# A two-layer decoder with 64 experts on one core: the second turn of a full half moves right behind the first gate/up product, and the weight refills are listed by the release of their rooms

## The chip, the cores and the metric

The kernel runs on one core of a Trainium2 chip. The metric is the device time of one execution in microseconds (us); smaller is better. The core has a matrix engine (TensorE, PE in the rows; PEld is its weight loads), a vector engine (VectorE, DVE), a scalar engine (ScalarE, ACT) and SyncE (SP), which here issues nearly all transfers. A transfer (DMA) runs beside the engines.

## The reference

Two layers, each an attention (differential in layer 0, latent in layer 1) and then a mixture of experts over 256 tokens of width 1024. Attention is not touched by the change. Of the experts:

```python
def hier_moe(h, w_group, b_group, w_expert, b_expert, w_gate, w_up, w_down):
    ...
    g_w, g_idx = lax.top_k(p_group, 1)                       # 1 of 8 groups
    ...
    e_w, e_idx = lax.top_k(jax.nn.softmax(e_logits, axis=-1), TOP_K)   # 2 of its 8 experts
    ...
    def body(e, acc):                                        # all 64 experts, width 256
        hid = jax.nn.silu(t @ w_gate[e]) * (t @ w_up[e])
        return acc + combine[:, e, None] * (hid @ w_down[e])
```

Each expert has 3 MB of float32 weights (1 MB each of gate, up and down), so that the two layers read 384 MB of expert weights, nearly all that the kernel reads.

## The kernel before

**Halves.** A layer's 64 experts are worked through in 16 halves of four experts, t = 0 to 15 (`LAST` = 15). For a half, 32 token slots per expert are gathered by a product with a 0/1 matrix `sel` (`Gather.places` makes the matrix on DVE, `Gather.rest` multiplies, L1270, and scales the result into `xg`, L334). Then come the gate/up product of four experts side by side (`into`, L1323, 64 matmuls), silu on ACT (L1328) and a multiplication on DVE (L1330), two transposes (L1335), the down product (`out_of`, L1349, 32 matmuls), a copy out of PSUM (`taken`, L1381), and a product with the transposed, weighted `sel` that puts the rows back to their tokens (`back`, L1389, with four additions into `xs` on DVE, L1354). The gather of half t+1 stands ahead of the down product of half t, and the `back` of half t behind the gate/up product of half t+1.

**Full halves.** Where an expert of the half has more than 32 tokens, the half needs a second turn with the same weights for slots 33 to 64 (`second`, inside `full`). One bit for each half is computed on the chip and read into a register of every engine (`path`), and every engine branches on it once in a half (L1449). Bit 16 says that an expert has more than 64 tokens; then `long_way` does the half in another way. Its branch (L1406) stands inside `second`, so that only full halves come to it; with this input the long way is never taken, but its code is jumped over. A branch hint (`mark_branch_hint_location`) on PE announces the jump over `second` of the next half.

**Rooms and refills.** Weights live in 10 rooms of 2 MB in SBUF. A unit is what one room holds: units 3p and 3p+1 are gate and up of the two experts of pair p, unit 3p+2 is both down weights. Unit n lies in the room that unit n-10 had (`RING`). A half uses six units: for half t, 6t, 6t+1, 6t+3, 6t+4 (gate/up) and 6t+2, 6t+5 (down). `order` lists the units to be loaded; `free(units)` says in the program that rooms are given up, and issues from `order` on SP as long as the head of the list has its room. SP's queue is in order: a transfer whose room is still in use holds up all behind it. Before the change `free` of the gate/up units stands in both ways of the branch on `path`: behind the second turn's gate/up product in a full half, and behind the down product in the others (where the transfers wait for the gate/up matmuls alone). `free` of the down units stands at the half's end.

Of the kernel before, what the change touches and what calls it, by code (L numbers as in the profile page):

```python
# [69 lines left out]
def trunk_kernel(  # L70
# [22 lines left out]
    def temp(cols):  # L93
        return work.tile([128, 512], F32, name="temp", bufs=3)[:, 0:cols]
# [1199 lines left out]
    def moe(layer, front):  # L1294
# [31 lines left out]
        def hidden(gu, weight=None):  # L1326
            sil, hid = temp(256), temp(256)
            ACT.activation(sil, gu[:, 0:256], AF.Silu)  # L1328
            if weight is None:
                DVE.tensor_mul(hid, sil, gu[:, 256:512])  # L1330
            else:
                DVE.scalar_tensor_tensor(hid, sil, weight, gu[:, 256:512], op0=OP.mult, op1=OP.mult)  # L1332
            tp = psum_bank()
            for k in range(2):
                PE.transpose(tp[:, 128 * k:128 * k + 128], hid[:, k::2], ident)  # L1335
            hdT = work.tile([128, 3, 128], F32, name="aT0")[:, 0:2, :]
            ACT.copy(hdT.rearrange("p k t -> p (k t)"), tp[:, 0:256])  # L1337
            return hdT
# [65 lines left out]
        def second(t, j, multiplied):  # L1404

            with tc.If(path >> 16):  # L1406
                long_way(t, j)
            this = Gather(front, j)
            this.places(t, 1)
            this.rest()  # L1410
            this.weighted(t)
            gu = into(t, j)
            ACT.copy(selT[:, 1 - j], this.turned())
            multiplied()
            y = out_of(t, hidden(gu))
            back(taken(y, lambda: temp(512)), selT[:, 1 - j])
# [21 lines left out]
        order[2:8] = order[3], order[4], order[2], order[6], order[7], order[5]  # L1438
        state = {"next": 0, "free": set()}
        def full(t, path, done):  # L1440

            mark = dict(state)

            def at_once():

                state.update(mark)
                done()

            with tc.If((path >> t) & 1, preferred_fallthrough_block=True, label=f"full{layer}_{t}") as more:  # L1449
                second(t, t % 2 if t < LAST else (t + 1) % 2, at_once)  # L1450
            with more.Else():
                at_once()
                if t < LAST:
                    tc.mark_branch_hint_location(f"full{layer}_{t + 1}", "LikelyTaken", engines=[PE.engine])

        this, ts = front.first, None
        with tc.manual_schedule(engines={e.engine for e in (PE, ACT, DVE)}):
            for t in range(LAST + 1):
                g, _, pairs = halves_of(t)
                if t == LAST:  # L1460
                    back(ts, selT[:, (t + 1) % 2])
                    full(t, path, lambda: None)

                    rows, weight = temp(256).bitcast(F32R).rearrange("p (b t) -> p b t", b=2), small("sums", 1)
                    this.weighted(t, sel[:, (t + 1) % 2])
                    ACT.copy(rows, this.turned())
                    DVE.tensor_reduce(weight, this.turned(sel[:, (t + 1) % 2]), axis=AX.XY, op=OP.add)
                    y = out_of(t, hidden(into(t, t % 2), weight), 4, lambda y, n: back_last(y, n - 1, rows) if n else None)
                    back_last(y, 3, rows)
                    free(units(g, pairs, "gu") | units(g, pairs, "d"))  # L1470
                    break
                gu = into(t, t % 2)
# [3 lines left out]
                hdT = hidden(gu)  # L1476
# [4 lines left out]
                ts = taken(y, lambda: prob().rearrange("p a t -> p (a t)")[:, 0:512])  # L1481
                if t + 1 < LAST:
                    this.weighted(t + 1)
                if t == 0:
                    path = nc.values_load(front.path[0:1, 0:1], min_val=0, max_val=2 ** 17 - 1)
                full(t, path, lambda: free(units(g, pairs, "gu")))
# [82 lines left out]
```

## Time and profile before

| | |
|---|---|
| median of 3 runs | 1233.47 us (1233.05 to 1235.77) |
| the profiled execution | 1237.15 us, of which the span is 1235.3 us |
| PE busy | 996.9 us, 81% of the span |
| DVE, ACT busy | 422.4 us, 229.1 us |
| read from HBM | 433.03 MB |
| mean granted TensorE clock | 0.924 of full |

A row of the timeline gives start, length, engine, line, operation, output and inputs, shape, count, and in brackets how long the engine sat idle before it and what ended that. A float32 matmul is recorded twice. SPq is SP's queue: its rows are the issue of transfers, which then run by themselves. PEq, PEldq and DVEq are the sequencers of PE and DVE.

### The profile page before, as it was taken

To read this page: it belongs to the slowest core of one execution; us is meant where nothing else is said; L and a number is where in the kernel's file an instruction comes from. 1 tells how busy PE (TensorE), PEld (TensorE's weight loads), DVE (VectorE), ACT (ScalarE), POOL (GpSimd) and SP (SyncE) were. 2 spreads that over 40 slices of the span, in tenths; PEclk is the share of its full clock that TensorE was granted. 3 is DMA by queue.
4 is the path that set the end of the run, shared out by engine and by line. 5 is a ranking of instruction groups with operands and counts; after the bars stand their busy time and mean duration, and the time that the engine had idled before them with its cause. 6 is when DMAs were issued, how large, how long until landed. Compare 5 with 4: busy or idle time off the path is not lost. (4 is left out here: it accounts for less than half of the span.)

```text
span 1235.3 us, 16593 instructions
## 1 busy us (share of the span) xinstructions
PE 996.9 (81%) x6544; PEld 552.7 (45%) x6544; DVE 422.4 (34%) x996; ACT 229.1 (19%) x594; POOL 1.3 (0%) x23
## 2 busy tenths in 40 slices
PE   8998888777777777777888999787777777799776
PEld 8897744343333333333438777443233333343332
DVE  6897622221111111111318876222111111122122
ACT  5565410000000000000016874000000000001000
POOL 0000000000000000000000000000000000000000
PEclk9998999898988888888999999999888888899888
DMA  9456871999999999999943386999999999969994
GB/s 350 184 214 250 329 288 72 427 424 425 425 425 425 426 425 426 425 425 425 408 194 120 134 316 283 369 425 425 425 426 426 425 426 425 426 266 375 425 424 175
DMA packets 78007, 435.92 MB, mean 353 GB/s; under 512 B 6960, under 2 KB 23088, under 8 KB 30128
## 3 DMA queue, kind: packets, MB, share of 16 engines
q1 hardware_dynamic: 77728, 434.02, 85.2%
q8 instruction: 86, 1.41, 0.4%
q14 instruction: 49, 0.40, 0.1%
q10 hardware_dynamic: 144, 0.09, 0.0%
HBM read 433.03 MB, written 1.05 MB: 351 GB/s over the span
## 5 line engine op out<-in xcount | busy, mean ns | idle before, releaser
L1323 PE MATMUL bank<-room,areaC 128*32 128x512 f32 x2240 | 349.7, 701 | 154.2 <-DMA room<-in_moe_w_up_dram 108.3
L1323 PEld LDWEIGHTS bank<-room,areaC 128*32 128x32 f32 x2240 | 108.6, 126 | 389.9 <-issue 373.7
L1354 DVE TENSOR_TENSOR xs<-xs,bank 128x512 f32<-128x512 f32 (+1 forms) x148 | 96.9, 658 | 482.3 <-PE bank L1389 477.2
L1349 PE MATMUL bank<-room,aT 128*32 128x512 f32 (+1 forms) x1160 | 131.6, 583 | 2.5 <-ACT aT L1337 2.5
L1389 PE MATMUL bank<-prob,val 128*128 128x512 f32 x240 | 108.1, 593 | 1.9 <-DVEq L1449 1.9
L1473 ACT COPY val<-bank 128x256 f32<-128x256 f32 x30 | 11.2, 373 | 508.2 <-PE bank L1291 508.2
L422 PE MATMUL bank<-room,areaB 128*128 128x256 f32 (+3 forms) x544 | 86.6, 311 | 4.1 <-DVE room L390 2.7
L334 DVE TENSOR_TENSOR areaC<-bank,pack 128x512 f32<-128x512 f32 x70 | 48.4, 691 | 111.4 <-PE bank L1270 111.4
L422 PEld LDWEIGHTS bank<-room,areaB 128*128 128x128 f32 x544 | 76.3, 193 | 9.0 <-DVE room L390 3.2
L1270 PE MATMUL bank<-val,areaB 128*128 128x128 f32 x576 | 71.5, 284 | 7.6 <-PEq L1406 3.2
L1270 PEld LDWEIGHTS bank<-val,areaB 128*128 128x128 f32 x576 | 67.9, 197 | 10.7 <-issue 10.4
L1270 PE MATMUL bank<-val,areaA 128*128 128x128 f32 x544 | 66.9, 282 | 4.5 <-DVE lg L1182 1.9
L1349 PEld LDWEIGHTS bank<-room,aT 128*32 128x32 f32 x1160 | 35.3, 112 | 70.7 <-issue 62.0
L1270 PEld LDWEIGHTS bank<-val,areaA 128*128 128x128 f32 x544 | 63.6, 196 | 6.3 <-issue 6.0
L390 DVE TENSOR_TENSOR room<-room,room 128x2048 fp32r<-128x2048 f32 (+4 forms) x33 | 62.4, 1897 | 6.5 <-ACT room L388 6.5
L1389 PEld LDWEIGHTS bank<-prob,val 128*128 128x128 f32 x240 | 43.3, 190 | 46.7 <-issue 46.7
L388 ACT CAST room<-room 128x2048 fp32r<-128x2048 f32 (+4 forms) x33 | 51.9, 1589 | 16.7 <-PE bank L1323 8.0
L1381 DVE COPY prob<-bank 128x512 f32<-128x512 f32 x30 | 20.7, 691 | 87.3 <-PE bank L1349 87.3
L1335 PE MATMUL bank<-ident,temp 128*128 128x128 f32 x70 | 17.6, 334 | 40.5 <-DVE temp L1330 37.2
L1381 ACT COPY prob<-bank 128x512 f32<-128x512 f32 x30 | 17.6, 586 | 155.4 <-PE bank L1349 155.4
L422 PE MATMUL bank<-room,areaA 128*128 128x512 f32 (+1 forms) x176 | 43.9, 393 | 2.0 <-DVE areaA L692 2.0
L1335 PEld LDWEIGHTS bank<-ident,temp 128*128 128x128 f32 x70 | 11.0, 206 | 66.7 <-DVE temp L1330 61.5
(245 smaller groups left out, 748.7 us busy)
## 6 DMA issues: line engine op xcount, KB each, us to landing
room<-in_moe_w_gate_dram SPq DMA_DIRECT2D x124, 1024.0 KB, 17.8
room<-in_moe_w_up_dram SPq DMA_DIRECT2D x124, 1024.0 KB, 19.3
room<-in_moe_w_down_dram SPq DMA_DIRECT2D x122, 1024.0 KB, 19.6
room<-in_diff_w_in_dram SPq DMA_DIRECT2D x11, 1024.0 KB, 10.8
room<-in_diff_w_out_dram SPq DMA_DIRECT2D x2, 2048.0 KB, 9.3
room<-in_moe_w_gate_dram SPq DMA_DIRECT2D x8, 512.0 KB, 14.8
room<-in_moe_w_up_dram SPq DMA_DIRECT2D x8, 512.0 KB, 13.6
room<-in_moe_w_down_dram SPq DMA_DIRECT2D x8, 512.0 KB, 10.1
```

The costliest lines, as they stand in the source:

```text
L334: DVE.tensor_tensor(dst, tp, gain[:, k0:k0 + n, None].to_broadcast([128, n, dst.shape[2]]), op=OP.mult)
L388: step(c + name)(lambda f=f: f(hi().bitcast(F32R), w()))
L390: step(c + name)(lambda eng=eng: eng.tensor_tensor(lo().bitcast(F32R), w(), hi(), op=OP.subtract))
L422: PE.matmul(out, a[k][x_].bitcast(F32R), b[k][w_].bitcast(F32R), start=first and j == 0, stop=last and j == n - 1)
L1270: PE.matmul(self.ps[kk][:, k, :], self.front.xn[:, tb, 4 * kk + k, :], self.sel[:, tb, :], start=tb + k == 0, stop=tb == 1, skip_group_che ...
L1323: PE.matmul(gu[M * c:M * c + M], x(k, slice(M * c, M * c + M)), w[:, :, k, :], start=k == 0, stop=k == 7)
L1335: PE.transpose(tp[:, 128 * k:128 * k + 128], hid[:, k::2], ident)
L1349: PE.matmul(y[n][M * c:M * c + M], hdT[:, k, M * c:M * c + M], w[:, k, ns], start=first and k == 0, stop=last and k == 1, skip_group_check ...
L1354: DVE.tensor_add(xs[:, tb, ns], xs[:, tb, ns], acc)
L1381: (ACT.copy, DVE.tensor_copy)[n](t, y[n])
L1389: PE.matmul(acc, rows[:, tb, :], t, start=True, stop=True)
L1473: ACT.copy(selT[:, t % 2], this.turned())
```

## The change

Four things change in the mixture of experts, in both layers. The first half of `hidden` (silu and multiplication) becomes `hidden_rows`, the second half (transposes and copy) `hidden_columns`. In each half the branch on `path`, with `second` in it, now stands right behind the gate/up product and `hidden_rows`, and ahead of everything else of the half; its product rows wait in the spare columns of the tiles that hold the rows of the half before. In `second` the branch over the long way moves behind the second turn's gate/up product and gets an else part and a hint of its own; `multiplied()`, the `free` of the gate/up units, is in both parts. `order` lists each half's six refills by release, the four that wait for gate/up rooms first and the two that wait for down rooms behind them; before, only six entries near the start were permuted, in another way. In the last half the second turn stands behind the first gate/up product too, where it stood ahead of it.

```diff
+        def hidden_rows(gu, weight=None, hid=None):
+            sil, hid = temp(256), temp(256) if hid is None else hid
             ACT.activation(sil, gu[:, 0:256], AF.Silu)
...
+        def hidden_columns(hid):
             tp = psum_bank()
...
-        def second(t, j, multiplied):
-            with tc.If(path >> 16):
-                long_way(t, j)
+        def second(t, multiplied):
+            j = (t + 1) % 2
+            tc.mark_branch_hint_location(f"long{layer}_{t}", "LikelyTaken", engines=[PE.engine])
             this = Gather(front, j)
             this.places(t, 1)
             this.rest()
             this.weighted(t)
-            gu = into(t, j)
+            hid = hidden_rows(into(t, j), None, held[1][:, 512:768])
+            with tc.If(path >> 16, preferred_fallthrough_block=True, label=f"long{layer}_{t}") as more:
+                long_way(t, j)
+                multiplied()
+            with more.Else():
+                multiplied()
+            hdT = hidden_columns(hid)
             ACT.copy(selT[:, 1 - j], this.turned())
-            multiplied()
-            y = out_of(t, hidden(gu))
+            y = out_of(t, hdT)
             back(taken(y, lambda: temp(512)), selT[:, 1 - j])
...
-        order[2:8] = order[3], order[4], order[2], order[6], order[7], order[5]
+        for t in range(LAST - 1):
+            order[6 * t:6 * t + 6] = (order[6 * t + n] for n in (0, 1, 3, 4, 2, 5))
...
                 if t == LAST:
                     back(ts, selT[:, (t + 1) % 2])
-                    full(t, path, lambda: None)
...
-                gu = into(t, t % 2)
+                gu = into(t, t % 2)
+                hid = hidden_rows(gu, weight, held[0][:, 512:768])
+                if t == 0:
+                    path = nc.values_load(front.path[0:1, 0:1], min_val=0, max_val=2 ** 17 - 1)
+                full(t, path, lambda: free(units(g, pairs, "gu")))
...
                 ACT.copy(selT[:, t % 2], this.turned())
                 if t:
                     back(ts, selT[:, (t + 1) % 2])
-                hdT = hidden(gu)
+                hdT = hidden_columns(hid)
...
-                full(t, path, lambda: free(units(g, pairs, "gu")))
                 free(units(g, pairs, "d"))
```

**SP's queue, from the end of half 0 to the full way of half 1 in layer 0.** Each row is one transfer of 1 MB (or two), named by the room that it fills. Before:

```order
L147 DMA room_75<-in_moe_w_gate_dram 128x2048
L147 DMA room_75<-in_moe_w_up_dram 128x2048
L1449 REGISTER_ALU x2
L1449 COMPARE_AND_BRANCH
...
L147 DMA room_78<-in_moe_w_gate_dram 128x2048
L147 DMA room_78<-in_moe_w_up_dram 128x2048
L143 DMA room_1642<-in_moe_w_down_dram 128x2048 x2
L147 DMA room_76<-in_moe_w_gate_dram 128x2048
L147 DMA room_76<-in_moe_w_up_dram 128x2048
```

The same place now:

```order
L147 DMA room_75<-in_moe_w_gate_dram 128x2048
L147 DMA room_75<-in_moe_w_up_dram 128x2048
L147 DMA room_76<-in_moe_w_gate_dram 128x2048
L147 DMA room_76<-in_moe_w_up_dram 128x2048
L1465 REGISTER_ALU x2
...
L147 DMA room_78<-in_moe_w_gate_dram 128x2048
L147 DMA room_78<-in_moe_w_up_dram 128x2048
L143 DMA room_1642<-in_moe_w_down_dram 128x2048 x2
L147 DMA room_1736<-in_moe_w_gate_dram 128x2048
L147 DMA room_1736<-in_moe_w_up_dram 128x2048
L143 DMA room_69<-in_moe_w_down_dram 128x2048 x2
```

Room 76 (unit 15, free once half 0 has done its down product) stood behind room 78 (unit 16, which waits for half 1's last gate/up product) and now stands ahead of it; all four units that wait for half 1's gate/up rooms are issued together.

**DVE, half 1 of layer 0, a full half's way.** `prob` and `temp` are row tiles, `val` is `sel`, `areaC` is `xg`. Before:

```order
L1354 TENSOR_TENSOR xs<-xs,bank 128x512 x4
L1330 TENSOR_TENSOR temp<-temp,bank 128x256
L1262 TENSOR_TENSOR val<-slot_no,pos 128x256
L334 TENSOR_TENSOR areaC<-bank,pack_81 128x4x128 x2
L1381 COPY prob<-bank 128x512
L1285 TENSOR_TENSOR val<-val,wt 128x256
...
L1262 TENSOR_TENSOR val<-slot_no,pos 128x256
L334 TENSOR_TENSOR areaC<-bank,pack_81 128x4x128 x2
L1285 TENSOR_TENSOR val<-val,wt 128x256
L1330 TENSOR_TENSOR temp<-temp,bank 128x256
```

The same half now:

```order
L1333 TENSOR_TENSOR prob<-temp,bank 128x256
...
L1262 TENSOR_TENSOR val<-slot_no,pos 128x256
L334 TENSOR_TENSOR areaC<-bank,pack_81 128x4x128 x2
L1285 TENSOR_TENSOR val<-val,wt 128x256
L1333 TENSOR_TENSOR prob<-temp,bank 128x256
...
L1387 COPY temp<-bank 128x512
L1360 TENSOR_TENSOR xs<-xs,bank 128x512 x4
L1465 UNCONDITIONAL_BRANCH x2
L1360 TENSOR_TENSOR xs<-xs,bank 128x512 x4
L1262 TENSOR_TENSOR val<-slot_no,pos 128x256
```

The second turn's selection (the first L1262) came behind the additions of the half before, the first turn's multiplication and the next half's gather; now it follows the first turn's multiplication at once, and what it was behind comes after the second turn's own additions.

**PE, the last half of layer 1.** L1291 transposes `sel`, `room_...` are the weights. Before:

```order
L1389 MATMUL bank<-temp,val 128x512 x4
L1449 UNCONDITIONAL_BRANCH x2
L1291 MATMUL bank<-ident,val 128x128 x4
L1323 MATMUL bank<-room_78,areaC 32x512
...
L1335 MATMUL bank<-ident,temp 128x128 x2
L1349 MATMUL bank<-room_9947,aT_18007 32x256 x2
```

Now:

```order
L1465 COMPARE_AND_BRANCH
L1588 BRANCH_PREFETCH_HINT
L1270 MATMUL bank<-val,areaA 128x128 x16
...
L1395 MATMUL bank<-temp,val 128x512 x4
L1465 UNCONDITIONAL_BRANCH x2
L1341 MATMUL bank<-ident,prob 128x128 x2
L1291 MATMUL bank<-ident,val 128x128 x2
L1355 MATMUL bank<-room_10106,aT_18321 32x256 x2
```

The first turn's 64 gate/up matmuls stood behind the branch; they now stand ahead of it, and only the transposes and the down product follow.

## Rows read from the trace of the kernel before

**Rows 1.** The page, 40 equal slices: busy tenths of the transfer engines

```profile
DMA  9456871999999999999943386999999999969994
```

**Rows 2.** Windows: stretch, length, busy PE, PEld, DVE, ACT, POOL; clock, DMA share, GB/s

```profile
186.00:213.00 27.00, 22.76 (x174) 12.18 (x172) 8.38 (x15) 2.28 (x7) 0.00 (x0) 1.00 0.08 22
213.00:630.00 417.00, 320.38 (x2003) 137.80 (x2004) 84.99 (x145) 23.58 (x58) 0.00 (x0) 0.91 1.01 424
1098.00:1118.00 20.00, 16.38 (x148) 7.42 (x144) 3.88 (x8) 1.62 (x4) 0.00 (x0) 1.00 0.28 105
1118.00:1214.00 96.00, 76.35 (x468) 31.63 (x464) 24.17 (x40) 5.81 (x14) 0.00 (x0) 0.89 1.01 423
```

**Rows 3.** Waits, all engines: who waits for what, us in total, times, longest

```profile
PE bank L1323 <- DMA room<-in_moe_w_up_dram: 108.3, 38, 5.2
```

**Rows 4.** Timeline of SP's queue, layer 0, halves 0 and 1

```profile
176.47 0.33 SPq L147 DMA_DIRECT2D room<-in_moe_w_gate_dram  x1
176.89 0.38 SPq L147 DMA_DIRECT2D room<-in_moe_w_up_dram  x1
210.82 0.33 SPq L147 DMA_DIRECT2D room<-in_moe_w_gate_dram  x1
```

**Rows 5.** Timeline of PE, layer 0, half 1

```profile
185.46 0.44 PE L1291 MATMUL bank<-ident,val 128*128 128x128 f32 x2
...
200.00 3.81 PE L1270 MATMUL bank<-val,areaB 128*128 128x128 f32 x32 [1.81 <-DVE val L1262]
203.74 7.07 PE L1323 MATMUL bank<-room,areaC 128*32 128x512 f32 x64
```

**Rows 6.** Timeline of SP's queue, layer 1, around the full half

```profile
1113.87 0.33 SPq L147 DMA_DIRECT2D room<-in_moe_w_gate_dram  x1
...
1120.10 0.33 SPq L147 DMA_DIRECT2D room<-in_moe_w_gate_dram  x1
```

**Rows 7.** Timeline of PE, layer 1: the full half and the half behind it

```profile
1088.41 0.44 PE L1291 MATMUL bank<-ident,val 128*128 128x128 f32 x2
...
1106.78 7.07 PE L1323 MATMUL bank<-room,areaC 128*32 128x512 f32 x64
...
1116.45 3.64 PE L1349 MATMUL bank<-room,aT 128*32 128x512 f32 x32 [0.52 <-ACT aT L1337]
1120.02 3.70 PE L1389 MATMUL bank<-temp,val 128*128 128x512 f32 x8
1123.65 7.07 PE L1323 MATMUL bank<-room,areaC 128*32 128x512 f32 x64
...
1135.98 3.83 PE L1270 MATMUL bank<-val,areaA 128*128 128x128 f32 x32
1139.74 3.64 PE L1349 MATMUL bank<-room,aT 128*32 128x512 f32 x32
```

**Rows 8.** Groups by line: count, busy us, mean ns, idle before

```profile
L1262 DVE TENSOR_TENSOR val<-slot_no,pos 128x256 f32<-128x256 bf16 x33 | 13.8, 418 | 0.6 <-DVEq L1406 0.6
L1328 ACT ACTIVATE temp<-bank 128x256 f32<-128x256 f32 x35 | 13.6, 389 | 9.5 <-PE bank L1323 9.5
```

**Rows 9.** Branches by line: ns min/median/max, first and last start

```profile
L1449 PEldq COMPARE_BRANCH  x35: 79/344/6334, 169.9 to 1205.2; - x35
L1406 PEldq COMPARE_BRANCH  x3: 3222/3892/5872, 195.9 to 1098.8; - x3
```

**Rows 10.** Timeline of PE, the last half of layer 0 and of layer 1

```profile
604.78 3.67 PE L1389 MATMUL bank<-prob,val 128*128 128x512 f32 x8 [0.96 <-DVEq L1449]
611.61 3.81 PE L1270 MATMUL bank<-val,areaB 128*128 128x128 f32 x32 [3.16 <-PEq L1406]
643.30 0.50 PE L1335 MATMUL bank<-ident,temp 128*128 128x128 f32 x2 [2.22 <-DVE temp L1332]
...
1204.81 3.67 PE L1389 MATMUL bank<-prob,val 128*128 128x512 f32 x8 [0.96 <-DVEq L1449]
1211.59 1.08 PE L1291 MATMUL bank<-ident,val 128*128 128x128 f32 x4 [3.11 <-PEq L1449]
```

More of the change, by code (lines that the diff above doesn't have):

```diff
@@ L1449, in full @@
             with tc.If((path >> t) & 1, preferred_fallthrough_block=True, label=f"full{layer}_{t}") as more:
-                second(t, t % 2 if t < LAST else (t + 1) % 2, at_once)
+                second(t, at_once)
             with more.Else():
@@ L1454, in full, with kept @@
                     tc.mark_branch_hint_location(f"full{layer}_{t + 1}", "LikelyTaken", engines=[PE.engine])
-        this, ts = front.first, None
+        def kept():
+            return prob().rearrange("p a t -> p (a t)")
+        this, ts, held = front.first, None, [kept() for _ in range(2)]
         with tc.manual_schedule(engines={e.engine for e in (PE, ACT, DVE)}):
@@ L1459, in moe @@
                 g, _, pairs = halves_of(t)
+                weight = None
                 if t == LAST:
                     back(ts, selT[:, (t + 1) % 2])
-                    full(t, path, lambda: None)
-                    rows, weight = temp(256).bitcast(F32R).rearrange("p (b t) -> p b t", b=2), small("sums", 1)
+                    weight = small("sums", 1)
                     this.weighted(t, sel[:, (t + 1) % 2])
+                    DVE.tensor_reduce(weight, this.turned(sel[:, (t + 1) % 2]), axis=AX.XY, op=OP.add)
+                gu = into(t, t % 2)
[3 more added lines that the diff above has]
+                full(t, path, lambda: free(units(g, pairs, "gu")))
+                if t == LAST:
+                    rows = temp(256).bitcast(F32R).rearrange("p (b t) -> p b t", b=2)
+                    hdT = hidden_columns(hid)
                     ACT.copy(rows, this.turned())
-                    DVE.tensor_reduce(weight, this.turned(sel[:, (t + 1) % 2]), axis=AX.XY, op=OP.add)
-                    y = out_of(t, hidden(into(t, t % 2), weight), 4, lambda y, n: back_last(y, n - 1, rows) if n else None)
+                    y = out_of(t, hdT, 4, lambda y, n: back_last(y, n - 1, rows) if n else None)
                     back_last(y, 3, rows)
-                    free(units(g, pairs, "gu") | units(g, pairs, "d"))
+                    free(units(g, pairs, "d"))
                     break
-                gu = into(t, t % 2)
                 ACT.copy(selT[:, t % 2], this.turned())
@@ L1475, in moe @@
                     back(ts, selT[:, (t + 1) % 2])
[L1476 removed]
+                hdT = hidden_columns(hid)
                 this = Gather(front, (t + 1) % 2)
@@ L1480, in moe @@
                 y = out_of(t, hdT)
-                ts = taken(y, lambda: prob().rearrange("p a t -> p (a t)")[:, 0:512])
+                held = [kept() for _ in y]
+                ts = taken(y, iter([h[:, 0:512] for h in held]).__next__)
                 if t + 1 < LAST:
                     this.weighted(t + 1)
-                if t == 0:
-                    path = nc.values_load(front.path[0:1, 0:1], min_val=0, max_val=2 ** 17 - 1)
-                full(t, path, lambda: free(units(g, pairs, "gu")))
                 free(units(g, pairs, "d"))
```

5 lines of the change are left out of this document (3 added, 2 removed).

## The prediction

> **What bounds the kernel now.** I first looked at where the transfer engines pause, since most of the span is reading weights. The page's 40 slices show them full from the 8th to the 20th and from the 26th to the 39th, low before and between, which is attention, and with two dents at the experts, the 7th and the 36th slice [rows 1]. The windows give the level of the full stretches, 424 and 423 GB/s, and the depth of the dents: 22 GB/s from 186 to 213 us in layer 0, 105 GB/s from 1098 to 1118 us in layer 1 [rows 2]. In the full stretches PE waits for weights (108.3 us over 38 waits [rows 3]), so there the rate of the transfers is the time: 1 MB takes 1.0486 MB / 424 GB/s = 2.47 us, a room 4.9 us, a half's 12 MB 29.7 us. What a dent lost is 27 x (1 - 22/424) = 25.6 us and 20 x (1 - 105/424) = 15.0 us. Every microsecond of a dent that is filled should end the kernel one microsecond earlier, as long as transfers stay the bound behind it.
>
> What the dents are, the branch rows say: the branch of L1406 is reached by full halves only, three times, the first at 195.9, the last at 1098.8 us [rows 9]; the one between is the last half of layer 0 (PE's wait for it, at 611.61 [rows 10]). So the dents are the two full halves that have halves behind them. SP issues nothing between 176.89 and 210.82 us [rows 4]: its head is a refill that waits for the full half's second gate/up product, which ended then (203.74 + 7.07 [rows 5]). In layer 1 it is freed at 1113.87 in the same way [rows 6], 0.02 us behind the end of the product (1106.78 + 7.07 [rows 7]).
>
> **The change, part by part.**
>
> *Earlier release of the gate/up rooms.* Before, from the end of the first gate/up product to the refill are 210.82 - 185.46 = 25.4 us in layer 0 [rows 4, 5] and 1113.87 - 1088.41 = 25.5 us in layer 1 [rows 6, 7]: a back product, transposes, the next half's gather, the first down product, a jump, the second gather and product. Now only these stand between: silu 0.39, a multiplication of the size of the selection, 0.42, the selection itself 0.42 [rows 8], about 0.5 for the engines' branches (half of the 0.96 us that PE waits for DVE at a branch [rows 10]; the bounds are 0 and 0.96), a gather of 203.74 - 200.00 = 3.7 us, and 7.1 us of product [rows 5]. That is 12.5 us, so the release comes 12.9 and 13.0 us earlier.
>
> *Refills by release.* In layer 0 unit 15 (4.9 us of transfers), whose room is free by 176 us, goes ahead of unit 16, which waits. The transfers so run dry 4.9 us later. In layer 1, where before the list is plain, everything freed by the half ahead has been issued by the time that the full half starts, before as after: nothing there. But behind the release four rooms (8 MB, 19.8 us) instead of two are now ready.
>
> *What is late next: the down rooms.* They now wait for the second turn's end and then the rest of the first. From the second gate/up product's end: 2.6 us to the down product (1113.85 to 1116.45), 3.6 and 3.6 us for it and its back product (to 1120.02 and 1123.65 [rows 7]); then 1.0 for the join of the branch (the 0.96 us above); 0.4 for the transposed selection [rows 5]; 3.6 for the back product of the half before (the row of the same form); 0.4 for what its additions leave of the transposes, 1.0 until DVE has done these additions and the selection, 3.8 and 3.6 us for gather and down product [rows 7]. Sum 23.6. The 8 MB last 19.8, so a new gap of 3.8 us opens in each of the two full halves. It is 0 if PE can overlap the waits, and some 10 if each of the joins and jumps costs what they did at worst; I take 3.8. In the half behind, the four down megabytes (9.9 us) cover its 7.1 us gate/up product, which frees the next four rooms, so I see no third gap.
>
> Layer 0: 12.9 + 4.9 - 3.8 = 14.0 us of 25.6. Layer 1: 13.0 - 3.8 = 9.2 us of 15.0.
>
> *The last half.* In both layers the 0.96 us branch wait ahead of its back product goes [rows 10], and 1.5 us come in behind half 14's gate/up product, where PE must now wait for silu and multiplication ahead of the branch. In layer 0, whose last half is full, the 3.16 us jump and the 2.22 us wait for the multiplication go too, and 1.7 us (silu to selection, as above) and a 1.0 us join come: 0.96 + 3.16 + 2.22 - 1.5 - 1.7 - 1.0 = 2.1 us gained. In layer 1 the 3.11 us jump [rows 10] goes behind the gate/up product, to where PE waits for the multiplication anyway, and about 1.0 us of weighting on DVE that the jump had covered shows: 0.96 + 3.11 - 1.5 - 1.0 = 1.6 us gained. Either could be 0, or 4 if the clock is better there.
>
> *All other halves* get a wait of some 1.5 us behind the gate/up product. Their cover is the transfers: a half without waits takes 1139.74 + 3.64 - 1123.65 = 19.7 us of PE [rows 7], now 21.2, against 29.7 of transfers. This 8.5 us is also what lets PE, which leaves the full half later against its transfers than before, catch up within two or three halves. Without cover it would be 1.5 x 29, over 40 us. SP has more branches and copies of the same transfers; it takes one copy and waits for rooms anyhow.
>
> Sum: 14.0 + 9.2 + 2.1 + 1.6 = 26.9 us. The profiled execution, 1237.15 us with 1.85 outside its span of 1235.3, would become 1210.3. It lay 3.7 us above the median of the runs, 1233.47; from that the forecast is 1206.6 us.
>
> **The rivals.**
>
> *The jump over the long way still costs.* Its branch on PE took 3.2 to 5.9 us [rows 9], which left PE idle for 1.8 and 3.2 us [rows 5, 10]. It now has a hint, and hinted jumps on L1449 took 0.34 us at the median; but one of 6.3 is in that row too, and the last half's jump idled PE for 3.11 us although half 14 had hinted it. It would come behind the release of the gate/up rooms, so it only delays the down rooms: about 3 us in each of three full halves, 9 us in all, 1216. [...]
>
> *The wait moves to the down rooms in earnest.* My 23.6 us is a sum with short waits; two joins, and PE's half clock behind a pause, could make it 30. Then 6.4 us more are lost in both full halves: 1219. Against it: the rows of the second turn stood nearly without gaps before [rows 7].
>
> *No second gap.* If the rest of the half is done within the 19.8 us, 7.6 us more are gained: 1199.
>
> *The dent in layer 0 gives nothing.* If PE, later against its transfers, frees the rooms of the next halves too late, layer 0's 14 us come back as small gaps: 1221. The 8.5 us of cover for each half speak against it.
>
> [...]
>
> **How the numbers follow.** Chances: the forecast 0.60, with a range of its own from 1201 to 1212; the jump 0.14; the down rooms 0.11; no second gap 0.08; layer 0 without gain 0.03; slower 0.04. From 1197 to 1220 everything but the last two and the tails is inside, some 0.85; the bounds of the last half's terms move little in that. A measurement here can tell about 0.2% (2.5 us) from no change. Only the slower case ends above that, and I keep 0.01 for an effect that cancels: faster 0.95, same 0.01, slower 0.04.
>
> **What would show it.** In layer 0's full half the refill's issue should come some 12.5 us behind the first gate/up product's end, with a short pause of the transfers ahead of it (some 7 us) and another of about 4 ahead of the down refills; in layer 1 a first pause of 2 us and a second of 4. All stretches behind should stand at 424 GB/s again at once. PE's branch over the long way should take well under 1 us; if it takes 3 or more, the first rival holds. If the second pauses are 8 us or longer, it is the second rival. I would be wrong altogether if the windows behind a full half fell below 400 GB/s for more than one half, or if the halves that aren't full showed transfers waiting for rooms.

## The result and the profile after

The changed kernel takes 1192.87 us (median of 4 runs, 1190.08 to 1195.65), the kernel before 1233.26 us on the same chip (4 runs, 1232.5 to 1235.77): ratio 0.9669, 95% interval 0.9639 to 0.9699. That is 40.4 us faster. The direction was forecast, but the size was not: 26.9 us were expected, and the time lies 4 us below the range of 1197 to 1220 us. The profiled execution took 1190.08 us, with a span of 1188.3 us and a granted clock of 0.941.

First the transfers, as in [rows 1, 2]: the page's 40 slices, and the windows around the two full halves (same columns).

```profile
DMA  9556868899999999999954387999999999999996
```

```profile
186.00:213.00 27.00, 23.85 (x148) 10.67 (x144) 8.33 (x13) 2.94 (x7) 0.00 (x0) 0.94 0.79 320
185.00:200.00 15.00, 13.30 (x87) 4.23 (x76) 2.62 (x5) 1.61 (x4) 0.00 (x0) 0.89 0.76 297
208.00:220.00 12.00, 12.00 (x115) 4.94 (x114) 2.41 (x4) 0.59 (x1) 0.00 (x0) 1.00 0.69 266
213.00:610.00 397.00, 301.71 (x2006) 134.08 (x2002) 84.06 (x143) 23.68 (x56) 0.00 (x0) 0.93 1.01 421
1060.00:1078.00 18.00, 16.52 (x130) 7.13 (x130) 4.06 (x7) 1.61 (x4) 0.00 (x0) 1.00 0.95 396
1086.00:1098.00 12.00, 12.00 (x115) 5.30 (x118) 2.41 (x4) 0.58 (x1) 0.00 (x0) 1.00 0.89 352
1098.00:1172.00 74.00, 61.81 (x418) 29.52 (x414) 20.93 (x35) 5.14 (x12) 0.00 (x0) 0.95 1.01 422
```

Where 22 GB/s stood there are now 320, and the dent of layer 1 has left the slices. Each dent has become two short pauses, as forecast: in layer 0 they cost 15 x (1 - 297/424) = 4.5 us and 12 x (1 - 266/424) = 4.5 us, 9.0 in place of 25.6; in layer 1 1.2 and 2.0 us, 3.2 in place of 15.0. Behind them the rate is at its level at once.

SP's queue in layer 0 [rows 4] shows why: the refills that wait for the gate/up rooms are issued at 189.33 us, those for the down rooms at 213.70.

```profile
171.85 0.38 SPq L147 DMA_DIRECT2D room<-in_moe_w_up_dram  x1
189.33 0.34 SPq L147 DMA_DIRECT2D room<-in_moe_w_gate_dram  x1
...
192.45 0.90 SPq L143 DMA_DIRECT2D room<-in_moe_w_down_dram  x2
213.70 0.33 SPq L147 DMA_DIRECT2D room<-in_moe_w_gate_dram  x1
```

In layer 1 [rows 6] the two releases now are:

```profile
1069.69 0.33 SPq L147 DMA_DIRECT2D room<-in_moe_w_gate_dram  x1
...
1092.15 0.33 SPq L147 DMA_DIRECT2D room<-in_moe_w_gate_dram  x1
```

PE's timeline around the full half of layer 0 [rows 5], from the end of half 0's product to half 2's:

```profile
159.53 0.41 PE L1291 MATMUL bank<-ident,val 128*128 128x128 f32 x2 [1.71 <-PEq L1465]
...
165.63 1.05 PE L1270 MATMUL bank<-val,areaB 128*128 128x128 f32 x7 [2.65 <-issue]
166.60 3.64 PE L1355 MATMUL bank<-room,aT 128*32 128x512 f32 x32
170.06 7.05 PE L1323 MATMUL bank<-room,areaC 128*32 128x512 f32 x64
178.48 3.84 PE L1270 MATMUL bank<-val,areaB 128*128 128x128 f32 x32 [1.37 <-DVE val L1262]
182.25 7.07 PE L1323 MATMUL bank<-room,areaC 128*32 128x512 f32 x64
190.72 0.48 PE L1341 MATMUL bank<-ident,prob 128*128 128x128 f32 x2 [1.40 <-DVEq L1420]
```

The gain by stretches. Each number is the difference of two times in PE's timeline: the end of layer 0's first gate/up product (before 162.65, after 157.82), the end of half 14's (591.15, 569.21), the start of layer 1's first L330 (655.61, 627.55), the start of its first gate/up product (766.74, 737.88), the end of half 14's (1191.19, 1148.87) and the end.

| stretch, us | before | after | gained | forecast |
|---|---|---|---|---|
| to layer 0's first gate/up product | 162.7 | 157.8 | 4.8 | 0 |
| layer 0, to half 14 (full half) | 428.5 | 411.4 | 17.1 | 14.0 |
| layer 0, last half (full too) | 64.5 | 58.3 | 6.1 | 2.1 |
| attention of layer 1 | 111.1 | 110.3 | 0.8 | 0 |
| layer 1, to half 14 (full half) | 424.4 | 411.0 | 13.5 | 9.2 |
| layer 1, last half | 44.1 | 39.4 | 4.7 | 1.6 |

The first row is code that the change doesn't touch. The versions below, all with the same code there, took 156.2 to 160.3 us, so the 4.8 us belong to the profiled execution of before, which lay 3.9 us above the median of its 4 runs. (That of the changed kernel lay 2.8 us below its median, so the two profiles differ by 47.0 us and the medians by 40.4.) Without that row 42.2 us are gained where 26.9 were forecast. The experiments ask where the surplus is from. Each was timed beside the kernel before on the same chip, whose median there was 1233.29 to 1235.87 us.

### The profile page after: what moved, and what is told of

Read it like the earlier page. It is cut to its first block, busy times and chain, and to the rows that moved or that the text cites. A ratio compares the mean times of both kernels' runs of the same rounds, so it can differ in the third digit from the quotient of the medians.

```text
span 1188.3 us, 16712 instructions
## 1 busy us (share of the span) xinstructions
PE 964.3 (81%) x6544; PEld 542.3 (46%) x6544; DVE 425.1 (36%) x996; ACT 231.7 (19%) x594; POOL 1.3 (0%) x23
## 5 line engine op out<-in xcount | busy, mean ns | idle before, releaser
L1323 PE MATMUL bank<-room,areaC 128*32 128x512 f32 x2240 | 330.6, 674 | 110.3 <-DMA room<-in_moe_w_up_dram 110.3
L1323 PEld LDWEIGHTS bank<-room,areaC 128*32 128x32 f32 x2240 | 101.1, 122 | 329.3 <-issue 315.1
L1333 DVE TENSOR_TENSOR prob<-temp,bank 128x256 f32<-128x256 f32 x33 | 13.9, 421 | 391.5 <-ACTq L1465 197.9
L1395 PE MATMUL bank<-prob,val 128*128 128x512 f32 x240 | 110.3, 602 | 2.8 <-issue 1.7
L1331 ACT ACTIVATE temp<-bank 128x256 f32<-128x256 f32 x35 | 13.4, 383 | 485.4 <-PE bank L1323 485.4
L1355 PEld LDWEIGHTS bank<-room,aT 128*32 128x32 f32 x1160 | 34.8, 110 | 68.8 <-issue 60.8
L1291 PE MATMUL bank<-ident,val 128*128 128x128 f32 x74 | 15.0, 284 | 44.7 <-DVEq L1465 29.6
```

Of the source, the lines that this page charges most:

```text
L1291: PE.transpose(tp[:, tb, :], (self.sel if sel is None else sel)[:, tb, :], ident)
L1323: PE.matmul(gu[M * c:M * c + M], x(k, slice(M * c, M * c + M)), w[:, :, k, :], start=k == 0, stop=k == 7)
L1355: PE.matmul(y[n][M * c:M * c + M], hdT[:, k, M * c:M * c + M], w[:, k, ns], start=first and k == 0, stop=last and k == 1, skip_group_check ...
L1395: PE.matmul(acc, rows[:, tb, :], t, start=True, stop=True)
```

## The experiments

### Two parts, each alone

**The new list alone** (the kernel before with it):

```diff
-        order[2:8] = order[3], order[4], order[2], order[6], order[7], order[5]
+        for t in range(LAST - 1):
+            order[6 * t:6 * t + 6] = (order[6 * t + n] for n in (0, 1, 3, 4, 2, 5))
```

> The kernel before with the new list of refills alone. Theory A (the gain is the two dents of the transfers, and the early release of the gate/up rooms fills them): only unit 15, 4.9 us of transfers, comes ahead in layer 0's dent, so about 5 us faster than before, 1228 us. Rival B (the list does the main work, since four rooms instead of two are refilled at each release): at least 15 us faster, 1218 or less.

1236.55 us, ratio 1.0014 (0.9994 to 1.0034): no difference, where even the smaller expectation was a gain of 5. In the trace layer 0 up to half 14 did get shorter, 428.5 to 424.5 us, but its last half took 68.8 us in place of 64.5 and layer 1's attention 114.0 in place of 111.1. In that last half the clock was lower (0.90 over 588 to 640 us, against 0.97 over 596 to 648 before), and the gather behind the jump took 6.67 us where it took 3.81 [rows 10]:

```profile
603.56 6.67 PE L1270 MATMUL bank<-val,areaB 128*128 128x128 f32 x32 [3.17 <-PEq L1406]
```

The mean clock of all twelve runs of this version was low too, 0.908 to 0.913, where the seventeen runs of the kernel before beside it had 0.921 at the median. Why the clock was lower stays open.

**The moved block alone** (the changed kernel with the old list, the same edit the other way round):

> The changed kernel with the old list of refills. Theory A: the release still comes early, but only 4 MB (layer 1) or 6 MB (layer 0) are listed ahead of the first room that waits for the down product, so the second pause grows by about 10 us in both layers and unit 15's 4.9 us are lost: 18 to 22 us slower than the changed kernel, 1211 to 1215 us. Rival C (the early release by itself does it, the list only matters for unit 15): 5 us slower, 1198.

1212.51 us, ratio 0.982 (0.9788 to 0.9852), 22 us of the 40, inside the range of the theory that the list is what keeps the down rooms from holding up the queue. The pauses are large again (windows):

```profile
180.00:195.00 15.00, 13.33 (x120) 5.38 (x118) 2.14 (x4) 1.61 (x4) 0.00 (x0) 1.00 0.42 156
205.00:216.00 11.00, 11.00 (x106) 5.50 (x108) 2.40 (x4) 0.58 (x1) 0.00 (x0) 1.00 0.35 127
1094.00:1108.00 14.00, 13.11 (x101) 6.96 (x103) 5.49 (x9) 0.96 (x2) 0.00 (x0) 1.00 0.18 56
```

In layer 1 the second pause costs 14 x (1 - 56/424) = 12.2 us, against 2.0 with the new list: at the earlier release only the two rooms ahead of a down refill could be filled. In layer 0 the two pauses cost 9.5 and 7.7 us, against 4.5 and 4.5, so there the second did not grow by the 10 us that the theory said, and the total fits better than its parts. So list and block are worth 0 and 22 us alone and 40 together. Only some half of the 22 is in the stretches up to half 14: by the profiles the block alone gained 8.0 us there in layer 0 and 2.2 in layer 1, and 5.9 and 4.5 in the last halves, nearly what it gains there with the list. In the same two stretches the list alone gained 4.0 and lost 1.4, and both together gained 17.1 and 13.5.

### The branch over the long way

**Back ahead of the second turn**, without else part and hint:

```diff
-            tc.mark_branch_hint_location(f"long{layer}_{t}", "LikelyTaken", engines=[PE.engine])
+            with tc.If(path >> 16):
+                long_way(t, j)
...
-            with tc.If(path >> 16, preferred_fallthrough_block=True, label=f"long{layer}_{t}") as more:
-                long_way(t, j)
-                multiplied()
-            with more.Else():
-                multiplied()
+            multiplied()
```

> The changed kernel with the branch over the long way back at the head of the second turn, without hint and else part. If the jump costs what it did before (PE idle 1.8 to 3.2 us), the second turn and both releases come 2 us later in each of three full halves: 4 to 7 us slower than the changed kernel, 1197 to 1200. If the wait for silu, multiplication and selection hides the jump: no difference, 1193.

1198.08 us, ratio 0.9708 (0.9676 to 0.9741), 5.2 us above the changed kernel, as expected. The jump took 5.7 to 7.2 us each time, and PE was idle for 5.35 us ahead of layer 0's second gather.

**Without the hint alone** (the first line of that diff left out):

> The changed kernel without the hint for the jump over the long way. If the hint is what makes the jump short (0.34 us in the changed kernel), it takes 3 us or more again, behind the release of the gate/up rooms, and the down rooms come 1 to 3 us later in two full halves and the end of layer 0 too: 3 to 8 us slower than the changed kernel, 1196 to 1201. If not, the same 1193.

1190.76 us, ratio 0.9648 (0.9617 to 0.9679): no difference. The branch row of each, with the hint, ahead of the turn, and without the hint:

```profile
L1420 PEldq COMPARE_BRANCH  x3: 336/345/366, 186.7 to 1067.0; - x3
```

```profile
L1414 PEldq COMPARE_BRANCH  x3: 5710/5794/7179, 174.6 to 1062.1; - x3
```

```profile
L1419 PEldq COMPARE_BRANCH  x3: 434/457/4160, 188.5 to 1072.3; - x3
```

So the place and the else part took the cost away, not the hint: two of the unhinted jumps took 0.43 and 0.46 us. The third, 4.2 us, stood in the last half of layer 0 and did not show in the time. Which of place and else part it was, these two runs don't tell.

### Jumps that the forecast left out

**Half 0 without a branch**, in the kernel before:

```diff
+            if t == 0:
+                at_once()
+                tc.mark_branch_hint_location(f"full{layer}_1", "LikelyTaken", engines=[PE.engine])
+                return
             with tc.If((path >> t) & 1, preferred_fallthrough_block=True, label=f"full{layer}_{t}") as more:
```

> The kernel before, with no branch in half 0 of either layer: half 0 has no second turn in this version, and with this input needs none. It prices the jump of half 0, which the forecast left out: PE idle for 4.8 us ahead of half 1's gate/up product in layer 0, and that product in 8.8 us instead of 7.1. Theory A (this jump was on the path of layer 0's dent, and the change shortened it by coming to it earlier, which is the 3.1 us by which layer 0's term was too small): half 1's product ends 5 to 6.5 us earlier and so does the kernel, 1227 to 1229 us. Theory B (it is covered): 1232 to 1235 us.

1228.63 us, ratio 0.9973 (0.9953 to 0.9993), 4.8 us faster, as Theory A had it. In the profile layer 0 up to half 14 took 421.5 us in place of 428.5. Half 1's product, in the kernel before and here:

```profile
176.75 8.77 PE L1323 MATMUL bank<-room,areaC 128*32 128x512 f32 x64 [4.79 <-PEq L1449]
```

```profile
165.48 7.05 PE L1323 MATMUL bank<-room,areaC 128*32 128x512 f32 x64
```

**The last half of layer 1 without a branch**, in the kernel before:

```diff
                     back(ts, selT[:, (t + 1) % 2])
-                    full(t, path, lambda: None)
+                    if layer == 0:
+                        full(t, path, lambda: None)
```

> The kernel before, with no branch in the last half of layer 1 (that half then has no second turn, and with this input needs none). Before, its hinted jump was slow and left PE idle for 3.1 us, and the 64 matmuls behind it took 9.5 us at a granted clock of 0.74, against 7.2 us at 1.00 in the changed kernel. Theory A (this jump is the whole of what the end of layer 1 gained): 5 us less, 1227 to 1229 us, and the stretch from half 14's gate/up product to the end goes from 44.2 to about 39 us. Theory B (the product there waits for weights, or the clock is low there whatever stands ahead): at most 2 us less, 1231 us or more.

1229.6 us, ratio 0.9974 (0.996 to 0.9988), 3.7 us faster, between the two expectations; the last stretch went from 44.1 to 39.9 us, which is nearly all that the change gained there, and that is Theory A. The product behind the jump, in the kernel before, here, and in the changed kernel:

```profile
1212.61 9.50 PE L1323 MATMUL bank<-room,areaC 128*32 128x512 f32 x64
```

```profile
1206.14 7.29 PE L1323 MATMUL bank<-room,areaC 128*32 128x512 f32 x64
```

```profile
1167.74 7.19 PE L1323 MATMUL bank<-room,areaC 128*32 128x512 f32 x64
```

**The last half of the changed kernel in its old form**, second turn ahead of the first gate/up product:

```diff
                 if t == LAST:
                     back(ts, selT[:, (t + 1) % 2])
+                    full(t, path, lambda: None)
...
-                full(t, path, lambda: free(units(g, pairs, "gu")))
+                if t < LAST:
+                    full(t, path, lambda: free(units(g, pairs, "gu")))
...
-                    free(units(g, pairs, "d"))
+                    free(units(g, pairs, "gu") | units(g, pairs, "d"))
```

> The changed kernel, with the last half of each layer as before: its second turn ahead of the first gate/up product. It prices the new form of the last half. Theory A (own milestones: 6.1 us in layer 0 and 4.7 us in layer 1 came from it, by a jump ahead of the product and the lower clock that the product had behind it): 1202 to 1204 us. Theory B (the forecast's 2.1 + 1.6 us, the rest being differences from one execution to the next): 1196 to 1197 us.

1194.5 us, ratio 0.9687 (0.9664 to 0.9711): below both expectations, on Theory B's side, and 2 us above the changed kernel, with intervals that overlap. Layer 0's last half took 61.6 us, 3.3 more than after, but layer 1's last stretch 39.7, as after. So in layer 1 the gain isn't the new form. PE did not wait for its jump there, although that stands ahead of the product as before: 1.53 us of idling ahead of the transposes, for DVE's weighting, in place of 3.11 us for its own sequencer, and the product took 7.20 us. What differs from before is the time between hint and branch. The hint for the last half stands in the else part of half 14's branch, which was at the end of half 14 and is now near its start. Rows of the kernel before, then of the changed one (the last start in each is that of layer 1's last half; the branches before are in [rows 9]):

```profile
L1564 PEldq BRANCH_PREFETCH_HINT  x28: 31/36/41, 176.2 to 1201.7; - x28
```

```profile
L1588 PEldq BRANCH_PREFETCH_HINT  x31: 31/31/45, 159.2 to 1146.0; - x31
L1465 PEldq COMPARE_BRANCH  x35: 79/422/5947, 155.5 to 1172.3; - x35
```

The lead was 1205.2 - 1201.7 = 3.5 us and is 1172.3 - 1146.0 = 26.3 us; in this version it was 17.7. Two runs of the kernel before tried the lead alone.

**Both hints in the else part of half 13:**

```diff
-                if t < LAST:
+                if t < LAST - 1:
                     tc.mark_branch_hint_location(f"full{layer}_{t + 1}", "LikelyTaken", engines=[PE.engine])
+                if t == LAST - 2:
+                    tc.mark_branch_hint_location(f"full{layer}_{LAST}", "LikelyTaken", engines=[PE.engine])
```

> The kernel before, with the hint for the last half's branch given one half earlier, in the else part of half 13 beside the hint for half 14. Before, that hint was executed at 1201.7 us and the branch at 1205.2 us, 3.5 us later, and the jump took 6.1 us; in the changed kernel 26.3 us lie between them (1146.0 and 1172.3 us), and the jump takes under 1 us. Theory A (it is the lead of the hint that the change lengthened, and two hints can be pending): the last half's jump takes under 1.5 us, the stretch from half 14's gate/up product to the end goes from 44.2 to about 40 us, the time to 1229 to 1230 us; in layer 0 the last half is full and nothing changes. Theory B (only one hint is kept): one of the two jumps, of half 14 or of the last half, takes some 6 us, and the time stays at 1232 to 1234 us. Theory C (the lead has nothing to do with it): the last half's jump still takes some 6 us and half 14's is as short as before.

1234.89 us, ratio 1.0 (0.9974 to 1.0026): no gain. The hint led by 33 us (1169.1 to 1202.5 us), and the last half's jump still left PE idle for 3.31 us; at half 14's PE waited 0.96 us for DVE, as before. That is the outcome of both Theory B and Theory C.

```profile
1209.17 1.09 PE L1291 MATMUL bank<-ident,val 128*128 128x128 f32 x4 [3.31 <-PEq L1449]
1210.19 9.41 PE L1323 MATMUL bank<-room,areaC 128*32 128x512 f32 x64
```

**Half 14 without a branch**, so that one hint leads by 29 us with no jump between:

```diff
+            if t == LAST - 1:
+                at_once()
+                tc.mark_branch_hint_location(f"full{layer}_{LAST}", "LikelyTaken", engines=[PE.engine])
+                return
             with tc.If((path >> t) & 1, preferred_fallthrough_block=True, label=f"full{layer}_{t}") as more:
```

> The kernel before, with no branch in half 14 of either layer (it then has no second turn, and with this input needs none). The hint for the last half stands at the head of the block behind half 13, so some 33 us ahead of its branch, and no other jump lies between, as it does in the changed kernel (26.3 us). Theory A (a hint acts if it has time and no other jump comes between): the last half's jump takes under 1.5 us, PE's idle time of 3.1 us ahead of the transposes goes, the 0.96 us at half 14's branch too, the stretch from half 14's gate/up product to the end of layer 1 goes from 44.2 to about 39 us, the time to 1227 to 1230 us. Theory C (it depends on where the code lies or on the transfers beside it): the jump still takes some 6 us, the stretch only loses the 0.96 us, the time is 1231 us or more.

1231.63 us, ratio 0.9956 (0.9931 to 0.9981), 4.2 us below the kernel before, which took 1235.87 us on that chip; the time by itself lies in Theory C's range, the difference and the rows are Theory A's. The last stretch went to 38.6 us. Hint, branch, and PE in the last half:

```profile
L1568 PEldq BRANCH_PREFETCH_HINT  x26: 31/36/41, 171.7 to 1172.4; - x26
L1453 PEldq COMPARE_BRANCH  x33: 79/339/6424, 165.5 to 1201.5; - x33
1205.02 0.41 PE L1291 MATMUL bank<-ident,val 128*128 128x128 f32 x2 [0.93 <-DVEq L1453]
...
1205.95 7.25 PE L1323 MATMUL bank<-room,areaC 128*32 128x512 f32 x64
```

PE no longer waits for its own sequencer, only 0.93 us for DVE's, and the product is at 7.25 us. With one hint, 29 us of lead and no jump between, this jump did not hold PE up; with 3.5 us of lead it did for 3.11 us, and with 33 us, another hint beside it and another jump between, for 3.31 us. Each of these edits moves the code as well, so that the place of the code has a part in it isn't ruled out.

**What the long jumps have in them** is in the traces. Beside the weights they show small transfers on queues called instruction. The view of transfers over the last half's jump of layer 1 in the kernel before (1205.19 to 1211.28 us) has one of 16 KB on queue q8:

```profile
q8 instruction: 1, 0.02, 1.0%
```

Over the same jump in the changed kernel (1172.28 to 1172.62 us) it has none. In the profiled executions of the two kernels such a transfer starts inside every one of PE's 14 branches that took 3 us or more (8 before, 6 after), and the branch ends 2.2 to 2.6 us behind its start; it starts inside none of the other 62, which took at most 1.2 us. That the jump waits for this transfer is not shown; the rows show that the two come together. Behind 53 of the 59 hints the next such transfer began 2.9 to 3.6 us later. In the kernel before the one behind the last hint came at 1204.8 us, 0.4 us ahead of the branch, and another fell into the jump, at 1208.9.

### Without second turns

Both kernels with the code of the full halves set to zero; the rows in slots 33 to 64 are not computed:

```diff
-            DVE.tensor_add(code, code, top)
+            DVE.tensor_tensor(code, code, code, op=OP.subtract)
```

> The kernel before, with the code of the full halves set to zero: no second turn is done, and the rows in slots 33 to 64 are left out. Beside the next run it shows what the change does outside the full halves. The dents (25.7 and 15.3 us by bytes) go, and some 23 us of second turn in the last half of layer 0: 1168 to 1174 us.

> The changed kernel with the same left out: no second turn, rows in slots 33 to 64 not computed. Theory A (outside the full halves the change gains only where a slow jump became a fast one, and that depends on where the code of the halves comes to lie): 2 to 8 us below the run above. Theory B (the forecast's terms for the last halves without a second turn, 1.6 us in each layer): 3 us below it. Rival C (the wait behind each gate/up product costs somewhere): the same or slower than the run above.

1173.87 us (ratio to the whole kernel before 0.9524, 0.9502 to 0.9546), inside what was expected, and 1165.53 us (0.9444, 0.9426 to 0.9462). So 8.3 us are gained with no full half at all, a little more than Theory A allowed and far more than the forecast's 3.2. By stretches they lie in the last halves: layer 0's went from 46.4 to 38.4 us and layer 1's from 44.2 to 39.5, while the two stretches up to half 14 changed by 0.2 and 1.6 us. Attention of layer 1 gave 4.2 us back (109.3 to 113.5). With full halves the change gained 40.4 us; the 32 us between hang on second turns, if the two parts add up, which is only roughly so: layer 0's last half gained 8.0 us here and 6.1 with its second turn.

### Further versions

**Gather behind the down product**, in the changed kernel:

```diff
                 this.places(t + 1, 0)
-                this.rest()
                 y = out_of(t, hdT)
                 held = [kept() for _ in y]
+                this.rest()
```

> The changed kernel, with the next half's gather product moved from ahead of the down product to behind it. Theory (what is left of the dents is the late down rooms): the down rooms come free one gather (3.8 us) and one wait for the selection (0.9 us) earlier, so the second pauses, 4.5 us in layer 0 and 2.1 us in layer 1, go, less some 0.5 us each, since PE now waits for the copy of the transposes with nothing to do: 1186 to 1188 us, against 1192.9. Rival (the pauses are set by the gate/up rooms of the half behind, or the regular halves lose their cover): 1192 us or more, with the windows behind the full halves below 420 GB/s.

1189.44 us, ratio 0.9644 (0.9621 to 0.9667), between the two expectations and with an interval that overlaps the changed kernel's. The second pauses went as expected (394 GB/s from 208 to 220 us, 427 from 1086 to 1098), and the stretches to half 14 lost 2.7 and 3.3 us. But layer 1's last stretch grew by 2.9, since half 14's jump, though hinted, left PE idle for 2.93 us, where in the changed kernel PE waited 1.33 us for DVE:

```profile
1147.90 0.66 PE L1291 MATMUL bank<-ident,val 128*128 128x128 f32 x2 [2.93 <-PEq L1465]
```

**Hints for half 0 and behind a full half**, in the changed kernel:

```diff
                 second(t, at_once)
+                if t < LAST:
+                        tc.mark_branch_hint_location(f"full{layer}_{t + 1}", "LikelyTaken", engines=[PE.engine])
...
+                if t == 0:
+                    tc.mark_branch_hint_location(f"full{layer}_0", "LikelyTaken", engines=[PE.engine])
                 gu = into(t, t % 2)
```

> The changed kernel, with a hint for the branch of half 0 (which has none, and leaves PE idle for 1.7 us and then 2.7 us in layer 0) and for the branch of the half behind a full one (3.7 us idle). The scheduler puts the hint for half 0 at the head of the block that ends in that branch, in layer 0 the head of the program, some 150 us ahead of it. Theory A (a hint that far ahead still acts): the first gate/up product of half 1 ends some 4 us earlier, the first pause of layer 0 (4.5 us) nearly goes, 1188 to 1189 us. Theory B (it does not act so far ahead): only the half behind a full one changes, which transfers cover: 1192 to 1193.5 us.

1192.32 us, ratio 0.9666 (0.9645 to 0.9688): the time is Theory B's, the stretch Theory A's. With the hint for half 0 PE no longer waited for its own sequencer behind half 0's product: it was idle there for 1.59 us, for DVE's, where the changed kernel has 1.71 us for its own and then 2.65. Half 1's product began at 166.77 us in place of 170.06, and layer 0 to half 14 took 407.1 us. What the hint behind a full half did is not shown. The gain came back elsewhere: 1.2 us in layer 0's last half, 2.6 in the attention behind it, 3.7 in layer 1's end, where half 14's jump left PE idle for 3.05 us. The attention's share may be chance: over the sixteen profiles, whose work there is the same, it took 109.3 to 114.0 us.

**The gather's move and the hint for half 0 together:**

> The changed kernel with two additions that each moved its own stretch in the runs above: the next half's gather product behind the down product, and a hint for the branch of half 0. Theory (the gains are in different pauses of the transfers and add up): layer 0 from the first gate/up product to that of half 14 goes from 411.4 us (changed kernel) to about 404 us (each alone 408.7 and 407.1), layer 1's stretch stays near 408, and the time is 1184 to 1187 us. Rival (the jump in the last half of layer 1 comes back slow, as it did in both versions, and takes 3 us): 1187 to 1190 us.

1193.69 us, ratio 0.9674 (0.9653 to 0.9695), above both expectations: they don't add up. Layer 0 to half 14 took 407.3 us, not 404, and half 14's jump in layer 1 left PE idle for 2.87 us. No version was shown to beat the changed kernel.

## Why the forecast was too small

**What held.** The release came 189.33 - 177.11 = 12.2 us behind the first product in layer 0 and 12.1 in layer 1, forecast 12.5. The down rooms came 24.4 and 22.5 us behind the second product (213.70 and 1092.15 us in SP's queue), forecast 23.6, so the second rival's 30 is out. The half clock behind a pause that it names is in the trace of before: 0.50 from 177 to 179 us, behind 4.79 us of idling. The second pauses were 4.5 and 2.0 us, forecast 3.8. The other halves paid nothing: the windows show 421 and 422 GB/s behind the full halves and a clock of 0.93 and 0.95, above that of [rows 2]. No run shows the slower kernel that the forecast gave 0.04. "No second gap" is out as well, and so is "the dent in layer 0 gives nothing": that stretch gained 17.1 us. The first rival did not come: the jump would still cost 5.2 us ahead of the second turn, but where it now stands it takes 0.34 to 0.37 us.

**Layer 0's full half, 17.1 against 14.0.** The step that failed is its starting point: everything ahead of half 1's first product was taken as unchanged. Half 0's branch has no hint, and its jump of 6.25 us left PE idle for 4.79 us ahead of that product, which then took 8.77 us at a clock of 0.82. With the branch earlier in half 0 the jump began while half 0's product still ran (155.5 us, against 157.8) and took 3.57 us; half 1's product was back at 7.05, at 1.00. From half 0's product to the end of half 1's were 185.53 - 162.65 = 22.9 us; now they are 177.11 - 157.82 = 19.3. These 3.6 us make the first pause 4.5 us in place of the forecast 7. Half 0 without its branch shows that they are on the path.

**Layer 1's full half, 13.5 against 9.2.** The terms that were mis-sized are the two pauses: they account for 15.0 - 3.2 = 11.8, since they were 0.8 and 1.8 us shorter than forecast. The other 1.7 us aren't seen in the pauses and stay open; the same stretch gained 1.6 us without any second turn, and versions with the old code there differ by up to 1.4 us (424.4 to 425.8).

**The last halves, 10.8 against 3.7.** This is the largest miss, beyond even the bound of 4 for either. The step that failed is the clock of the products behind the waits, which the sum put at nothing. In layer 1 PE's waits from half 14's product to the end shrank from 7.45 to 5.61 us: 1.8, near the forecast 1.6. The rest is the product behind the jump, 9.50 against 7.19 us, and the transposes ahead of it. Windows over that product, before (behind 3.11 us of idling and four transposes) and after:

```profile
1212.60:1222.10 9.50, 9.50 (x65) 2.27 (x64) 0.42 (x1) 0.11 (x1) 0.00 (x0) 0.74 0.29 111
```

```profile
1167.70:1175.00 7.30, 7.23 (x66) 3.53 (x64) 0.42 (x1) 0.03 (x1) 0.00 (x0) 1.00 0.86 330
```

The clock was 0.74 and is 1.00; in the four transposes ahead of the product it was 0.50 before. The forecast also moved the jump to a place where PE waits anyway and left it its length. That the jump, whose hint the move of half 14's branch also moved, shrank from 6.1 us to 0.34 was luck: at 6.1 us it would have ended at 1178.4, some 2.3 us behind the start of the transposes at 1176.07 (an estimate from these rows). In layer 0 the waits from half 14's product to the first L330 shrank from 13.3 to 9.4 us, 3.9 where 2.1 were forecast, and the first down products behind the last transposes, before and after, went from 3.51 us at a clock of 0.54 to 1.93 us at 1.00:

```profile
644.27 3.51 PE L1349 MATMUL bank<-room,aT 128*32 128x256 f32 x32 [0.46 <-ACT aT L1337]
```

```profile
618.09 1.93 PE L1355 MATMUL bank<-room,aT 128*32 128x256 f32 x32
```

No run takes the parts of layer 0's last half one by one: its old form gave back 3.3 of the 6.1 us, and the rest is read from the rows alone.

Surplus by these steps: 3.1 + 4.3 + 4.0 + 3.1, and 0.8 in attention, 15.3 us in the profiled executions; 13.5 by the medians.

**Still open:** why hinted jumps are sometimes long (5.95 us at 327.1 us in the changed kernel, with 30 us of lead, where the transfers run on at 425 GB/s; half 14's in the last three versions, with PE idle for 2.93, 3.05 and 2.87 us), although a 16 KB transfer began 3.2 us behind the hint of the one at 327.1 us, as behind those of short ones; and why the new list alone gives its 4 us back.

## What to carry to other kernels

A queue in order is worth what its head allows: up to half 14 of the two layers earlier release alone gained 8.0 and 2.2 us, a list by release alone 4.0 and -1.4, and both together 17.1 and 13.5, so cost such a pair as one edit. When a branch moves, list what its hint and its neighbours' hints are now ahead of; a jump on the path cost its own idle time here (3.11 us in the last half of layer 1) and, in some places, a lower clock of the product behind it (0.74 there, 9.50 us in place of 7.19). Count from the last point that the edit really leaves alone, not from the first that it is meant to change.

## What was not expected of the hardware

With a hint for half 0's branch, PE was idle behind half 0's product for 1.59 us in place of 1.71 and 2.65 us in the changed kernel; with a hint 3.5 us ahead the last half's jump of layer 1 took 6.1 us in the kernel before. In the traces of both kernels each of PE's 14 jumps of 3 us or more has a 16 KB transfer that starts inside it, and none of the 62 shorter ones has. An idle time of PE of some 3 us at the last half's jump of layer 1, with only four transposes behind it, was followed by 64 matmuls in 9.50 and 9.41 us in place of 7.2 (the kernel before, at a clock of 0.74, and with both hints early). But it isn't so everywhere: behind 3.16 us of idling in layer 0's last half the gather took its usual 3.81 us in the kernel before [rows 10], at a clock of 1.00, and 6.67 us with the new list alone.
